# Cosine-similarity attention on one core: norm sums of Q and K folded together on TensorE, the first pair taken head by head, new instruction orders

## The chip, the core and the metric

The kernel runs on one core of a Trainium2 chip. A core has five engines that run side by side, each through its own list of instructions in order: TensorE (PE, matrix products into PSUM), VectorE (DVE), ScalarE (ACT, functions such as the exponential), GpSimd (POOL) and SyncE (SP, which here only issues transfers). They wait for each other through semaphores. Transfers between HBM and the on-chip SBUF are issued by SP or ScalarE and run on 16 DMA engines. PSUM has eight banks of 512 float32 columns for 128 partitions. The metric is the time of one execution in microseconds, lower is better.

## The reference

Inputs Q, K, V are float32 of shape (8, 12, 512, 64): 8 batches, 12 heads, 512 rows of 64 numbers. tau is 0.1.

```python
Q_norm = Q / (np.linalg.norm(Q, axis=-1, keepdims=True) + 1e-10)
K_norm = K / (np.linalg.norm(K, axis=-1, keepdims=True) + 1e-10)
scores = np.einsum('bhqd,bhkd->bhqk', Q_norm, K_norm) / tau
weights = np.exp(scores - np.max(scores, axis=-1, keepdims=True))
weights = weights / (np.sum(weights, axis=-1, keepdims=True) + 1e-10)
return np.einsum('bhqk,bhkd->bhqd', weights, V).astype(np.float32)
```

Scores are cosines divided by 0.1, so they lie between -10 and 10 and the exponential needs no maximum taken off.

## The kernel before

The 96 heads are worked in 48 pairs. A head's 512 rows are laid out as 128 partitions with four rows each; these four blocks are counted t or c from 0 to 3. For a pair s:

- **Load**: Q, K and V, 256 KB each (pair 0's Q and K in halves by head). SP issues them, and for pair 0 ScalarE issues K.
- **Squares** of Q and K in one tile of 16 rows of 64 per partition. From pair 4 on GpSimd squares Q and K together in 1024 columns (L325); pairs 0 to 3 use ScalarE and GpSimd.
- **Sums of squares.** For K, TensorE adds eight products with the identity, each taking 8 of the 64 columns of the eight rows, so that 64 columns are left in PSUM (L342), and VectorE reduces these to 8 sums (L349). For Q, from pair 4 on, VectorE reduces 512 columns to 8 sums itself (L353). Pairs 1 to 3 use TensorE for both, pair 0 VectorE.
- **Inverse roots.** For pairs 0 to 3 ScalarE takes a logarithm and the exponential of minus half of it (L236, L240, L367, L370). Later pairs are taken in groups of 2 or 4, for which VectorE makes Newton steps in some eight small operations (L377 to L386).
- **Products**: Q by its inverse roots on VectorE, K on GpSimd, for ten pairs on VectorE too (L404). Eight **transposes** on TensorE (L410) and one copy on VectorE (L417) give `qt`.
- **Scores**: for each block c of K two matmuls of 512 columns, one per head, into two of the four score banks (L446). **Exponentials**: one ScalarE instruction of 1024 columns per block, with the factor 1/tau as its scale, into `et` (L469). The two pairs of banks take turns, so a score waits for the exponential before the previous one.
- **Values**: V is cast to bf16 with a column of ones (L474); 32 matmuls of 65 columns give the sums and the denominators (L486); VectorE takes a reciprocal and a product (L497, L499), SP stores 256 KB (L503).

For pair 0 each step is made for each head by itself, up to half-size exponentials for blocks 0 and 1. For pair 47 the last block's exponential comes in three pieces (`PIECES`: head 0 whole, head 1's blocks 0 and 1, head 1's blocks 2 and 3; L460), and each piece has its own values, reciprocal, product (L514, L525, L527) and store (L531).

The order is written out by hand. Each operation is added to a list with its engine, what it needs and a due time, and `ORDER` gives, for each engine, the operations' numbers in the order in which it carries them out. Due times had a part in finding the orders; when the kernel is built only `ORDER` counts. An engine's instructions wait for what they need and hold up all that stand behind them in the same list. A negative number in TensorE's list is a matmul without use (L188) of so many columns, and eight others (L185) come first.

Of the kernel before, what the change touches and what calls it, by code (L numbers as in the profile page):

```python
# [8 lines left out]
class Op:  # L9
    def __init__(self, key, eng, kind, due, needs, emit, slot=None):  # L10
        self.key, self.eng, self.kind, self.due, self.emit = key, eng, kind, due, emit
        self.needs, self.slot = [n for n in needs if n is not None], slot
        self.own = False
        self.sem, self.val, self.inc, self.used = None, 0, 0, False
        self.start = self.end = None


class Program:


    def __init__(self, nc):
        self.nc, self.ops, self.list = nc, {}, []

    def add(self, key, eng, kind, due, needs, emit, **kw):
        assert key not in self.ops, key
        op = Op(key, eng, kind, due, needs, emit, **kw)
        self.ops[key] = op
        self.list.append(op)
        return op

# [7 lines left out]
    def dummy(self, columns):  # L38
        return Op("dummy", "pe", "", 0, [], lambda e: self.fill(e, columns))

    def run(self):
        nc = self.nc
        order = self.schedule()
        dma_sems, dma_count, last_out = {}, {}, {}
        for e, ops in order.items():
            for o in ops:
                o.waits = [self.ops[n] for n in o.needs]
                if e in ("pe", "act") and not o.own:
                    o.waits = [p for p in o.waits if p.eng != e]
                for p in o.waits:  # L50
                    p.used = True
        for e, ops in order.items():
# [14 lines left out]
        def write(engine, name):  # L67
            seen = {}
            for o in order[name]:
                want = {}  # L70
                for p in o.waits:
                    k = id(p.sem)
                    if p.val > max(seen.get(k, 0), want.get(k, (None, 0))[1]):
                        want[k] = (p.sem, p.val)
                for k, (sem, val) in want.items():
                    engine.wait_ge(sem, val)
                    seen[k] = val
# [29 lines left out]
def bass_cosine_similarity_attention_kernel(  # L107
# [15 lines left out]
    R_QK, R_V, R_SQ, R_QN, R_QT, R_ET, R_O, R_X = RINGS  # L123

# [13 lines left out]
    xs = {g: sb(f"xs{g}", [128, 64], f32) for g in NORM_ON_ACT}  # L138
# [9 lines left out]
    t_k0 = sc_ps[:, 3, :].bitcast(bf16)[:, 0:SEQ].rearrange("p (t x) -> p t x", t=NT)  # L148
    n_ps = nc.alloc_psum_tensor("nps", [128, R_X, 160], f32)

    P = Program(nc)

# [20 lines left out]

    P.add("one", "pool", "one", -100, [], lambda e: e.memset(ones[:, :], 1.0))
    P.add("eye", "pool", "sm_pool", -99, ["one"], lambda e: e.affine_select(  # L175
        out=ident[:, :], in_=ones[:, :], pattern=[[1, 128]], base=0, channel_multiplier=-1,
        compare_op=ALU.is_equal, fill=0.0))
    P.add("eps", "pool", "sm_pool", -98.5, [], lambda e: e.memset(eps[:, :], 1e-19))
    P.add("table", "act", "table", -900, [], lambda e: e.preload_act_table_set("natural_log_exp_and_others"))
    P.add("vone", "pool", "vone", -98, [], lambda e: e.memset(  # L180
        vb[:, :, :, :, DIM : DIM + 1].rearrange("p r c h o -> p (r c h o)"), 1.0))

    def warm(e):
        for k in range(WARM):
            last = e.matmul(out=o_ps[1][:, :], lhsT=ident[:, :], rhs=warm_in[:, :], start=True, stop=True)  # L185
        return last

    P.fill = lambda e, n: e.matmul(out=sc_ps[:, 0, 0:n], lhsT=ident[:, :], rhs=warm_in[:, 0:n], start=True, stop=True)  # L188
    P.add("wz", "dve", "sm_dve", -100, [], lambda e: e.memset(warm_in[:, :], 0.0))
    P.add("warm", "pe", "warm", -100, ["eye", "wz"], warm)  # L190

    def due_sq(s):
        g = group[s]
        return START + PERIOD * first[g] - 7.6 + (1.9 if g in NORM_ON_ACT else 0) - 3.43 * (first[g] + sizes[g] - 1 - s) - slack(s, M_SQ)

    def due_red(s):
        return due_sq(s) + 2.0

    slots = sorted((START + PERIOD * (s + 1) + 0.9 * PV_AT[4 * h + 3] + 0.05 + late(s), s, h) for s in range(NP - 1) for h in range(2))
    session, attached, early = {}, {}, []  # L200
    for s, w in sorted(((s, w) for s in range(NP) for w in range(2) if on_pe(s, w)), key=lambda j: (due_red(j[0]), j)):
        at = due_red(s) + 0.3
        if s < EARLY:
            early.append((s, w))
            continue
        due, i, h = next(x for x in slots if x[0] >= at and (x[1], x[2]) not in attached)
        attached[i, h] = (s, w)
        session[s, w] = (h, due, [("PV", i, h, NT - 1)])
    before = [[], []]
    for s, w in sorted(early):  # L210
        session[s, w] = (w, due_red(s), before[w])
        before[w] = [("RED", s, w)]
    bank_free = {}
    for s in range(NP):
        for h in range(2):
            bank_free[s, h] = before[h]
            before[h] = [("NRM", s, h)] + ([("RED",) + attached[s, h]] if (s, h) in attached else [])

    def head0(TF):
        for h in range(2):  # L220
            at = -100 + h
            x4 = [xs[0][:, 8 * w + 4 * h : 8 * w + 4 * h + 4] for w in range(2)]
            for w in range(2):
                src_, dst = qk[0][:, w, h, :], sq[0][:, 8 * w + 4 * h : 8 * w + 4 * h + 4, :]
                flat = dst.rearrange("p g d -> p (g d)")
                if SQ0[w][h] == "act":
# [467 lines left out]
```

## Time and profile before

| what | value |
|---|---|
| median of three runs | 190.92 us (190.64 to 191.05) |
| span of the profiled execution | 188.7 us |
| what lies between that span and the median | 2.2 us |
| first exponential starts | 8.08 us |
| busy: ScalarE, TensorE, VectorE, GpSimd | 182.1, 176.0, 164.9, 155.0 us |
| exponentials (L469) | 193 in 175.8 us |
| data moved | 50.75 MB, mean 269 GB/s |

The span runs from the first to the last instruction of one profiled execution; the runs that give the median were not profiled. The execution that was profiled has no other time on record than its span. In the timeline, rows begin with start and duration in microseconds, then engine, line, operation, output and inputs; equal instructions in a row are merged. What stands in brackets is idle time of the engine before the row and what ended it. Matmuls and exponentials overlap their successors, so the distance between starts tells more than the durations.

### The profile page before, as it was taken

What the parts mean: (1) busy time and instruction counts of PE and PEld (TensorE: products, weight loads), DVE (VectorE), ACT (ScalarE), POOL (GpSimd) and SP (SyncE); (2) the same over time, 40 slices, a digit from 0 to 9 for tenths busy, and PEclk for the clock granted to TensorE, in tenths of its full rate; (3) what the DMA queues carried; (4) which work ended last, traced back from release to release, by engine and by line L of the source; (5) the groups of instructions that cost most, each with busy time, mean ns of one, the idle gap of its engine ahead of it and who ended that gap; (6) DMA issues with size and microseconds to landing.
All of it is one profiled execution on the core that took longest, in us unless ns stands there. A gap on an engine that the chain in (4) does not pass through costs nothing.

```text
span 188.7 us, 6679 instructions
## 1 busy us (share of the span) xinstructions
PE 176.0 (93%) x2726; PEld 110.1 (58%) x2726; DVE 164.9 (87%) x530; ACT 182.1 (96%) x214; POOL 155.0 (82%) x145
## 2 busy tenths in 40 slices
PE   6998999999999999999999999999999999899992
PEld 2555666566665666566666566665666556555552
DVE  2789999999999899999999989998889987977543
ACT  4899999999999999999999999999999999999992
POOL 5689999999999999999999899999699898260000
PEclk9999999999999999999999999999999999999999
DMA  4999999999999978999898997997999943113133
GB/s 153 345 352 351 349 357 322 311 315 377 381 385 354 296 264 261 349 335 299 270 255 256 378 344 233 300 314 223 280 326 336 326 139 113 59 56 115 56 114 111
DMA packets 52445, 50.75 MB, mean 269 GB/s; under 512 B 3136, under 2 KB 52416, under 8 KB 52416
## 3 DMA queue, kind: packets, MB, share of 16 engines
q1 hardware_dynamic: 51984, 50.02, 81.6%
q8 instruction: 21, 0.34, 0.7%
q10 hardware_dynamic: 432, 0.33, 0.5%
q14 instruction: 8, 0.07, 0.1%
HBM read 37.75 MB, written 12.58 MB: 267 GB/s over the span
## 4 chain that ended last, share of the span: by engine, by line
ACT 94%; DMA 3%; SPq 1%; issue 1%; DVE 1%; PE 0%
ACT et L469 92%; DMA qk<-in_Q_dram 3%; SPq L299 0%; SPq L296 0%; ACT et L460 0%; DVE ob L527 0%; ACT sq L317 0%; ACT ys L367 0%; ACT nps L370 0%; PE ops L514 0%; DVE rd L525 0%
## 5 line engine op out<-in xcount | busy, mean ns | idle before, releaser
L469 ACT ACTIVATE et<-scps 128x1024 bf16<-128x1024 f32 (+1 forms) x193 | 175.8, 1247 | 0.0
L325 POOL TENSOR_TENSOR sq<-qk 128x1024 bf16<-128x1024 f32 x44 | 82.7, 1891 | 2.0 <-DMA qk<-in_K_dram 2.0
L446 PE MATMUL scps<-qt 64*128 64x512 bf16 x384 | 75.5, 385 | 7.4 <-ACT et L469 2.3
L486 PE MATMUL ops<-vb,et 128*128 128x65 bf16 x1504 | 74.5, 194 | 0.0
L486 PEld LDWEIGHTS ops<-vb,et 128*128 128x128 bf16 x1504 | 56.1, 98 | 27.9 <-issue 21.5
L404 POOL TENSOR_TENSOR qn<-qk,rk 128x512 bf16<-128x512 f32 x37 | 38.1, 1041 | 6.4 <-DVE rk L382 6.1
L499 DVE TENSOR_TENSOR ob<-ops,rd 128x256 f32<-128x256 f32 x94 | 39.3, 420 | 0.9
L404 DVE TENSOR_TENSOR qn<-qk,nps 128x512 bf16<-128x512 f32 x57 | 38.1, 678 | 0.4 <-ACT nps L370 0.4
L417 DVE COPY qt<-tps 128x1024 bf16<-128x1024 bf16 x47 | 32.3, 688 | 4.1 <-PE tps L410 3.4
L446 PEld LDWEIGHTS scps<-qt 64*128 64x128 bf16 x384 | 19.4, 92 | 26.1 <-ACT et L469 10.1
L410 PE MATMUL tps<-ident,qn 128*128 128x128 bf16 x376 | 33.0, 221 | 0.1
L474 POOL TENSOR_SCALAR vb<-vf 128x512 bf16<-128x512 f32 x48 | 29.3, 624 | 0.7 <-PE tps L410 0.7
L353 DVE TENSOR_REDUCE nps<-sq 128x8 f32<-128x512 bf16 x44 | 29.7, 683 | 0.0
L410 PEld LDWEIGHTS tps<-ident,qn 128*128 128x128 bf16 x376 | 21.4, 98 | 12.0 <-issue 5.7
L497 DVE RECIPROCAL rd<-ops 128x4 f32<-128x4 f32 x94 | 16.6, 177 | 9.2 <-PE ops L486 5.8
L342 PE MATMUL ops<-sq,ident 128*128 128x64 bf16 x400 | 20.0, 193 | 0.0
L342 PEld LDWEIGHTS ops<-sq,ident 128*128 128x128 bf16 x400 | 14.9, 98 | 4.1 <-issue 2.9
L349 DVE TENSOR_REDUCE nps<-ops 128x8 f32<-128x64 f32 x44 | 9.3, 211 | 0.8 <-PE ops L342 0.7
L377 DVE TENSOR_TENSOR nps<-nps,ys 128x32 f32<-128x32 f32 (+1 forms) x30 | 6.3, 208 | 0.2
L378 DVE SCALAR_TENSOR_TENSOR nps<-nps,ys 128x32 f32<-128x32 f32 (+1 forms) x30 | 6.2, 207 | 0.2
L185 PE MATMUL ops<-warm_in,ident 128*128 128x512 bf16 x8 | 3.6, 631 | 1.4 <-POOL ident L175 1.4
L319 POOL TENSOR_TENSOR sq<-qk 128x512 bf16<-128x512 f32 (+1 forms) x4 | 3.7, 933 | 1.2 <-DMA qk<-in_K_dram 1.0
(50 smaller groups left out, 40.8 us busy)
## 6 DMA issues: line engine op xcount, KB each, us to landing
vf<-in_V_dram SPq DMA_DIRECT2D x48, 256.0 KB, 5.3
qk<-in_Q_dram SPq DMA_DIRECT2D x47, 256.0 KB, 4.3
qk<-in_K_dram SPq DMA_DIRECT2D x47, 256.0 KB, 5.4
out_dram<-ob SPq DMA_DIRECT2D x47, 256.0 KB, 3.5
qk<-in_Q_dram SPq DMA_DIRECT2D x2, 128.0 KB, 2.7
qk<-in_K_dram ACTq DMA_DIRECT2D x2, 128.0 KB, 2.9
out_dram<-ob SPq DMA_DIRECT2D x1, 128.0 KB, 1.7
out_dram<-ob ACTq DMA_DIRECT2D x1, 64.0 KB, 1.6
```

The source lines that it names most:

```text
L325: lambda e: e.tensor_tensor(out=sqf, in0=data, in1=data, op=ALU.mult))
L342: last = e.matmul(out=o_ps[bank][:, 320:384], lhsT=ident[:, :], rhs=sq[iqs][:, 8 * w : 8 * w + 8, 8 * k : 8 * k + 8], start=(k == 0), stop ...
L353: lambda e, w=w, dst=dst: e.tensor_reduce(out=dst, in_=sq[iqs][:, 8 * w : 8 * w + 8, :], axis=AX.X, op=ALU.add))
L404: lambda e, w=w, r=r: e.tensor_tensor(out=qn[iqn][:, w].rearrange("p t h d -> p h t d"), in0=qk[iq][:, w].rearrange("p h (t d) -> p h t d" ...
L410: last = e.transpose(t_ps[:, w, t, :], qn[iqn][:, w, t].rearrange("p h d -> p (h d)"), ident[:, :])
L417: lambda e: e.tensor_copy(out=qt[iqt][:, :, :, :].rearrange("p w t x -> p (w t x)"), in_=t_ps[:, :, :, :].rearrange("p w t x -> p (w t x)")))
L446: last = e.matmul(out=sc_ps[:, 2 * b + h, :], lhsT=qt[iqt][64 * h : 64 * h + 64, 1, c, :], rhs=qt[iqt][64 * h : 64 * h + 64, 0, :, :], sta ...
L469: lambda e, c=c, b=b, hs=hs: e.activation(out=et[iet][:, c, hs[0] : hs[-1] + 1, :], in_=sc_ps[:, 2 * b + hs[0] : 2 * b + hs[-1] + 1, :], f ...
L474: lambda e: e.tensor_scalar(out=vb[:, iq, :, :, 0:DIM].rearrange("p c h d -> p h c d"), in0=vf[iv][:, :, :].rearrange("p h (c d) -> p h c ...
L486: last = e.matmul(out=o_ps[h][:, 65 * t : 65 * t + 65], lhsT=et[iet][:, c, h, 128 * t : 128 * t + 128], rhs=vb[:, iq, c, h, :], start=(c = ...
L497: lambda e, h=h, grid=grid: e.reciprocal(out=rd[io][:, h, :], in_=grid[:, :, DIM]))
L499: lambda e, h=h, grid=grid: e.tensor_tensor(out=ob[io][:, h], in0=grid[:, :, 0:DIM], in1=rd[io][:, h, :].unsqueeze(2).to_broadcast([128, N ...
```

## The change

- **Sums of squares**: for all pairs from 2 on, TensorE adds sixteen products with the identity, each taking 4 of the 64 columns of all sixteen rows of Q and K, and VectorE makes one reduction of 64 columns to 16 sums. The reductions of 512 columns on VectorE are gone. Pair 1, and pair 0 but for head 0's Q, keep eight products for each sum.
- **Pair 0**: head 0 first. Its Q's square is in two halves, on VectorE and ScalarE; its Q is multiplied by the roots and transposed in halves. Its K is only cast to bf16 and transposed as it is (`raw`); the cast multiplies K by 10 (1 over tau), and K's inverse root enters as the scale of the exponentials, one number per partition. Head 0's first block has two exponentials of 256 columns, the other three one of 512 each; head 1 has two of 1024, of two blocks each. Pair 1 is also written in this way (`EARLY`).
- **Loads**: of pair 0 only head 0's K stays on ScalarE's queue, head 1's K goes to SP as the third load; K of pair 1 goes to ScalarE's queue, behind the table load.
- **Products of K** on VectorE for 20 pairs instead of ten. The square of pair 5 is on VectorE.
- **Order**: all of `ORDER` is new. The matmuls without use are gone, but for the first eight, which now take their weights from a zeroed tile and so don't wait for the identity. On ScalarE the square of pair 1's Q stands ahead of the first exponential, that of pair 2's Q behind four of pair 0's seven. In pair 47 ScalarE takes the last block's pieces in the order head 0, head 1 first half, head 1 second half; before, head 1's first half came first. VectorE handles head 1's first half, head 0, head 1's second half, as before.
- **Waits** that other waits imply are left out.

```diff
-                    for k in range(8):
-                        last = e.matmul(
-                            out=o_ps[bank][:, 320:384], lhsT=ident[:, :], rhs=sq[iqs][:, 8 * w : 8 * w + 8, 8 * k : 8 * k + 8],
-                            start=(k == 0), stop=(k == 7))
+            for k in range(16):
+                last = e.matmul(
+                    out=o_ps[bank][:, 320:384], lhsT=ident[:, :], rhs=sq[iqs][:, :, 4 * k : 4 * k + 4],
+                    start=(k == 0), stop=(k == 15))
...
-                P.add(("RED", s, w), "dve", "red", due_red(s) + 0.5 * w, [*sqs, ("NRMS", 0, 0, 1), *new(g - R_X), *last_direct(s)],
-                      lambda e, w=w, dst=dst: e.tensor_reduce(
-                          out=dst, in_=sq[iqs][:, 8 * w : 8 * w + 8, :], axis=AX.X, op=ALU.add))
+        P.add(("RED", s), "dve", "redp", [("SSQ", s)] + ([] if acts else [*free["n"], *new(g - R_X)]),
+              lambda e: e.tensor_reduce(
+                  out=x2[:, :, c8 : c8 + 8], in_=o_ps[bank][:, 320:384].rearrange("p (w g e) -> p w g e", w=2, e=4), axis=AX.X, op=ALU.add),
...
+                scale = xs[s][:, 16 + 8 + 4 * hs[0] + cs[0] : 16 + 8 + 4 * hs[0] + cs[0] + 1] if one else inv_tau
+                return e.activation(out=o, in_=i, func=ACT.Exp, scale=scale)
...
+                    emit = lambda e, o_=o_, i_=i_: e.tensor_scalar(out=o_, in0=i_, scalar1=inv_tau, scalar2=1.0, op0=ALU.mult, op1=ALU.mult)
+                kind, needs = "cast", lds
...
+EARLY = {0: {'heads': True,
+     'queue': {(0, 0): 'sp', (1, 0): 'act', (0, 1): 'sp', (1, 1): 'sp'},
...
+     'items': (((0,), (0,), 0, 256, 0),
+               ((0,), (0,), 256, 512, 1),
+               ((0,), (1,), 0, 512, 2),
+               ((0,), (2,), 0, 512, 3),
+               ((0,), (3,), 0, 512, 0),
+               ((1,), (0, 1), 0, 512, 2),
+               ((1,), (2, 3), 0, 512, 0))},
+ 1: {'heads': False,
...
+     'queue': {0: 'sp', 1: 'act'},
...
-K_ON_DVE = (1, 2, 3, 4, 9, 15, 21, 27, 33, 39)
+K_ON_DVE = (2, 3, 4, 6, 9, 11, 13, 15, 17, 19, 21, 23, 25, 27, 29, 31, 33, 35, 37, 39)
...
+ ('SQ', 5, 2): 'dve'}
...
     "act": (
-        "9 10 3 12 25 16 18 17 29 31 67 30 68 106 44 74 75 40 41 45 112 47 113 49 82 150 84 151 86 88 120 122 124 126 "
+        "9 4 62 14 24 16 17 30 64 31 38 48 43 39 54 56 70 50 71 117 52 60 121 122 58 81 157 79 158 85 83 129 131 "
...
-        "1717 1719 1747 1749 1751 1753 1781 1783 1785 1788 1787 1789 1804 "
+        "1616 1669 1671 1673 1675 1696 1698 1700 1702 1723 1725 1727 1729 1750 1752 1754 1756 1757 1758 1773 "
```

In the first line of the new ScalarE list 64 is the square of pair 1's Q, 48 the first exponential, 117 the square of pair 2's Q; at the end 1756 to 1758 are the three pieces, which were 1787 to 1789.

## The prediction

> **What bounds the kernel now.** The page first, its busy times and the chain that ended last.
>
> ```profile
> PE 176.0 (93%) x2726; PEld 110.1 (58%) x2726; DVE 164.9 (87%) x530; ACT 182.1 (96%) x214; POOL 155.0 (82%) x145
> ACT 94%; DMA 3%; SPq 1%; issue 1%; DVE 1%; PE 0%
> ```
>
> ScalarE (ACT) carries 94% of the chain. Busy shares on TensorE mislead: its rows overlap. Then the chain in order of time.
>
> ```profile
> 2.67 4.85 DMA qk<-in_Q_dram
> 7.55 0.63 ACT sq L317
> 8.18 0.48 ACT et L469
> ...
> 14.79 169.56 ACT et L469 x185
> 184.34 0.78 ACT et L460 x2
> 185.12 0.05 issue
> 185.16 0.31 PE ops L514 x4
> ```
>
> The middle has no gap: 185 exponentials, 169.56 / 185 = 0.917 us each, from 14.79 to 184.34. Nothing shortens that stretch unless an exponential gets cheaper. A change can gain before 14.8 and after 184.3, and it can lose in between by making ScalarE wait. So I read the head and the tail in the timeline, ScalarE alone.
>
> ```profile
> 6.06 0.63 ACT L317 ACTIVATE sq<-qk 128x512 bf16<-128x512 f32 x1
> 6.60 0.16 ACT L240 ACTIVATE nps<-ys 128x4 f32<-128x4 f32 x1
> 6.83 0.42 ACT L317 ACTIVATE sq<-qk 128x256 bf16<-128x256 f32 x1
> 7.55 0.63 ACT L317 ACTIVATE sq<-qk 128x512 bf16<-128x512 f32 x1 [0.30 <-DMA qk<-in_Q_dram]
> 8.08 0.58 ACT L469 ACTIVATE et<-scps 128x512 bf16<-128x512 f32 x1
> 8.56 0.30 ACT L367 ACTIVATE ys<-xs,eps 128x16 f32<-128x16 f32 x1
> 8.89 0.19 ACT L370 ACTIVATE nps<-ys 128x16 f32<-128x16 f32 x1
> ```
>
> The first exponential starts at 8.08, behind squares that wait for loads: Q of pair 1 (below: Q1) is in at about 6.04, its K (K1) at 6.81, Q of pair 2 at 7.52 (single events of the trace). Starts give each operation's pitch: a square of 512 columns 0.54 (6.06 to 6.60), a 512-column exponential 0.48 (8.08 to 8.56), a logarithm 0.20 but 0.33 when its own root follows at once (8.56 to 8.89), a root 0.11, a 1024-column exponential 0.90, a 256-column one 0.26 (183.98 to 184.24). Pair 1's first exponential starts at 12.55; from there both kernels have the same ScalarE work.
>
> For the end, the timeline of VectorE:
>
> ```profile
> 184.95 0.17 DVE L525 RECIPROCAL rd<-ops 128x2 f32<-128x2 f32 x1 [0.72 <-PE ops L514]
> 185.15 0.29 DVE L527 TENSOR_TENSOR ob<-ops,rd 128x128 f32<-128x128 f32 x1
> 185.50 0.18 DVE L525 RECIPROCAL rd<-ops 128x4 f32<-128x4 f32 x1
> 185.71 0.42 DVE L527 TENSOR_TENSOR ob<-ops,rd 128x256 f32<-128x256 f32 x1
> 186.06 0.16 DVE L525 RECIPROCAL rd<-tps 128x2 f32<-128x2 f32 x1
> 186.25 0.29 DVE L527 TENSOR_TENSOR ob<-tps,rd 128x128 f32<-128x128 f32 x1
> ```
>
> The first reciprocal and product belong to head 1's first piece, whose exponential ran first of the last three; they are over before the last exponential's results arrive, and only two of the three pieces stand behind it.
>
> **The sums, VectorE and GpSimd.** In the groups, 44 reductions of Q on VectorE go (L353, 683 ns each, 29.7 us busy). Ten more K products come to VectorE (L404, 678 ns, 6.8 us), one 1024-column square (about 1.2 by the same row), and GpSimd loses ten products of 1041 ns and that square (1891). VectorE ends some 20 us lighter, GpSimd 12 us. (A pair's one remaining reduction reads 64 columns as before, 211 ns.) Neither is on the chain, so worth nothing on the path; the cover is the unbroken row of exponentials.
>
> **The sums, TensorE.** Eight sum matmuls per pair become sixteen, spaced 0.029 in the trace: +0.23 per pair. TensorE's need per pair by spacing: four score pairs 0.32 each, 32 value matmuls at 0.030, eight transposes at 0.056, eight sums: 2.9 of 3.67 us (four exponentials); it becomes 3.15. On average it fits, but a score may only start once ScalarE has freed its banks, so what counts is the work put between two scores: 0.917 - 0.32 = 0.59 per gap, beyond which scores run late. By rows, a score pair starts 0.06 after the exponential that frees its banks, takes 0.39, the next starts 0.04 later and lasts at least 1.03: 1.52 of two periods (1.83), so 0.32 of lateness is free. Counting the new list, gap by gap: the old had no gap over 0.59; the new one has some of 0.94. Before pair 4's first score stand 12 + 20 value matmuls (0.94), eight transposes (0.45), then 32 sum matmuls (0.93): lateness 0.35, 0.20, 0.53. That is 0.2 over. Four other places reach 0.35, 0.03 over each, inside the error. Taken +0.20; bounds 0 (sums ready early, weights counted high) and +0.45 (each of the waits on VectorE in those gaps adding 0.05).
>
> **The head.** What the new lists do on ScalarE after the loads: half of the first head's Q square, K's square, logarithm, root, logarithm of K, then the 512-column square of pair 1's Q, root, logarithm of head 1, first exponential (256 columns). The first scores need only head 0: Q's logarithm at about 4.3, root 4.6, products and two copies on VectorE (0.29 to 0.42 each) to 6.2, score to 6.5. So the square, in line ahead, decides: first exponential = Q1's landing + 0.02 + 0.54 + 0.11 + 0.20 = landing + 0.87. Q1 is now fourth on SP's queue, behind K's second half (128 KB, 0.35 us at the 358 GB/s of the stretch from 5.6 to 8 us), and K1 leaves SP for ScalarE's queue, where its issue (0.47) stands behind the table load (1.28) and is over by 3.0, ahead of the first data at 3.39. Bounds of the landing: 5.6 (the 220 GB/s between 3.5 and 5.6 filled by the second queue) and 6.81 (Q1 and K1 both in only when the second was before). Taken 6.2, half the 0.35 after 6.04, nearest to the row of the same transfer. First exponential 7.07, 1.0 earlier.
>
> From there to pair 1's first exponential ScalarE does 2 x 0.26 + 3 x 0.48 + 2 x 0.90 of exponentials, two roots 0.22, pair 1's logarithm and root 0.31, the square of pair 2's Q 0.54 (it stood before the first exponential), pair 2's logarithm and root 0.44 back to back: 5.27, where the old had 12.55 - 8.08 = 4.47. So 7.07 + 5.27 = 12.34: the gain shrinks from 1.0 to 0.21. Bounds -0.5 (landing 5.6; then pair 3's norms, whose loads end near 10.75, are late next) and +0.4. What could break the row: K's square for pair 1 on GpSimd (1.04) and head 1's K product (0.61) behind it, 6.81 + 1.65 = 8.5 at the latest; transposes and copy to 9.4, needed at about 10. The raw K costs one cast on GpSimd (about 0.4) instead of a product, its root is an operand of five exponentials; I take no price for that.
>
> The semaphore waits left out as implied, and the fill matmuls (L188), cost nothing on the chain.
>
> **The tail.** The new list runs head 0's exponential first, then head 1's two pieces, but VectorE still normalises head 1's first piece first. That piece is in 0.26 before the last, its reciprocal about 0.33 after its end (as 185.11 to 185.50 with four matmuls, here two), that is 0.06 after the last end, and 0.42 later head 0's reciprocal: 0.48 after, against 185.50 - 185.39 = 0.11 now. All that follows (products, stores on SP) shifts by +0.37. Bounds 0.1 (the last store waiting for the one before it on SP) and 0.45.
>
> **Sum.** -0.21 + 0.20 + 0.37 = +0.36 on the span of 188.7. The three runs' median is 190.92, 2.2 above that span; I carry this over: 191.3. A change of 0.2% (0.38 us) is about what a measurement can tell from none, so this stands at the edge.
>
> **Rivals.** (1) Q1 lands late. For: the two queues shared the engines in turn for pair 0 (landings 3.39, 3.58, 3.94, 4.22, SP and ScalarE alternating). If Q1 and K1 share likewise, Q1 lands near 6.8, +0.6: 191.9. Against: in that stretch the engines were only 0.69 busy.
> The Trainium skill ("DMA: Bandwidth & Descriptors", section "Queues, rings and completion order") says each engine goes round-robin between the queue rows it has work for; by that rule Q1 and K1 finish together and the sum is this rival's. The alternating landings agree with it.
> (2) TensorE stays slow longer. The eight first matmuls take 0.43 us each (3.60 for the row below) and only at about 5.2 the fills' spacing halves.
>
> ```profile
> 1.44 3.60 PE L185 MATMUL ops<-warm_in,ident 128*128 128x512 bf16 x8 [1.44 <-POOL ident L175]
> 4.82 0.78 PE L188 MATMUL scps<-warm_in,ident 128*128 128x256 bf16 x4
> ```
>
> Without fills the speed-up may come a like stretch later, near 9: two single scores (0.21 each) and late transposes, about +0.5: 191.8.
> The Trainium skill ("TensorE: Matmul & The Clock Gate", section "What's actually happening") has the clock released after a busy window that runs freely, which no row here can place.
> (3) Head hides it: the landing is early or pair 4's score in time: 190.9, no change.
> (4) Faster: the pace itself. Exponentials start 0.903 apart while ScalarE is fresh (from 14.66 on) and settle at 0.917; if that is VectorE's traffic, 20 us less of it could give 0.91: 185 x 0.007 = 1.3, so 190.0. It decides below 0.913. Against: from 100 to 180 us VectorE and GpSimd are already lighter, and the pace is the same 0.917.
> (5) The change's lists stall elsewhere (TensorE waiting for sums or products in line before a score): 0.3 each, 192 and more.
>
> **Chances.** Forecast 0.40 (191.0 to 191.6, half on each side of the 0.2% bound), (1) 0.17, (2) 0.08, (3) 0.18, (4) 0.10, (5) 0.07. Faster 0.10; same 0.20 + 0.18 = 0.38; slower 0.52. The range 190.4 to 192.3 leaves out most of (4) and (5).
>
> **What would show it.** First exponential near 7.1 and pair 1's first near 12.3; 46 groups of 16 sum matmuls; a start held back by TensorE near 23 us; after the last exponential the first L525-like reciprocal of head 0 at +0.5 instead of +0.1. Wrong if exponentials show idle time in several places, if their pace differs from 0.917, or if Q1 lands outside 5.6 to 6.8.

## The result and the profile after

The changed kernel takes 200.46 us (median of four runs, 199.59 to 201.24), the kernel before 190.97 beside it (190.64 to 191.05): 1.0500 times as long, 95% interval 1.0469 to 1.0532. The forecast was 191.3, from 190.4 to 192.3. It was wrong by 9 us. Some executions of a kernel came out 1.5% or more above its fastest; each time below is the median of the others, with their range. The profiled execution of the changed kernel took 201.24 us with a span of 199.5, against 188.7 before: 10.8 us to be found.

From its page, the busy times, the chain by engine, and the group of the exponentials (busy time, mean ns of one, then idle time before them and what ended it):

```profile
PE 184.7 (93%) x3097; PEld 121.4 (61%) x3097; DVE 157.5 (79%) x508; ACT 186.0 (93%) x215; POOL 141.9 (71%) x132
PE 42%; ACT 33%; DMA 9%; POOL 6%; DVE 5%; SPq 2%; issue 1%; POOLq 0%
L288 ACT ACTIVATE et<-scps 128x1024 bf16<-128x1024 f32 x192 | 178.5, 1034 | 6.2 <-PE scps L270 5.2
```

ScalarE had 94% of the chain and has 33%; TensorE, with only 8.7 us more of busy time than before, leads. ScalarE now waits 5.2 us for scores where its row had no gap, and its busy time grew by 3.9 us: exponentials that start late overlap less.

The chain in order of time, the changed kernel:

```profile
2.16 4.04 DMA qk<-in_Q_dram
6.22 0.63 ACT sq L320
...
24.87 18.60 ACT et L288 x20
45.13 0.47 PE ops L651 x12
...
69.64 1.05 PE ops L531 x32
71.01 0.59 PE ops L651 x16
71.93 0.60 PE ops L651 x16
...
121.83 4.19 DMA qk<-in_K_dram
126.16 1.90 POOL sq L321
128.05 1.01 POOL qn L618
129.83 0.47 PE ops L651 x12
...
158.24 4.20 DMA vf<-in_V_dram
162.51 0.62 POOL vb L638
163.13 1.01 POOL qn L618
166.13 29.43 ACT et L288 x33
```

It can be read in three stretches. The exponentials bind in short stretches to about 50 us. Then groups of work on TensorE (sums L531, values L651) stand in the chain one after another, each between two scores. From about 108 us the chain leaves TensorE and goes back through GpSimd to loads: a K load ends before a square, and right behind that square a K product goes off; the same again with a V load and its cast. From 166 us ScalarE is unbroken to the end.

How far the same exponential ends later than in the kernel before (two profiled executions, worked out from single instructions) puts sizes to the stretches. I call this the lag. After 1, 5, 13, 23, 35, 37, 41 and 47 pairs it is 0.28, 1.04, 1.59, 3.19, 5.85, 8.82, 10.31 and 10.44 us; the tail adds 0.34. So some 5.5 us are lost slowly up to pair 35, and 4.5 in a few steps between pairs 35 and 41. The granted clock was 0.50 from 146.0 to 149.4, inside the largest of these steps (2.74 us at one pair); the last section comes back to this.

The head and the end of ScalarE, timeline of the changed kernel:

```profile
6.22 0.63 ACT L320 ACTIVATE sq<-qk 128x512 bf16<-128x512 f32 x1 [0.61 <-DMA qk<-in_Q_dram]
7.04 0.47 ACT L288 ACTIVATE et<-scps,xs 128x256 bf16<-128x256 f32 x1
7.41 0.17 ACT L409 ACTIVATE nps<-ys 128x4 f32<-128x4 f32 x1
7.67 1.27 ACT L288 ACTIVATE et<-scps,xs 128x512 bf16<-128x512 f32 x2
8.82 0.30 ACT L392 ACTIVATE ys<-xs,eps 128x16 f32<-128x16 f32 x1
...
11.96 1.92 ACT L288 ACTIVATE et<-scps 128x1024 bf16<-128x1024 f32 x2
...
194.49 1.34 ACT L288 ACTIVATE et<-scps 128x512 bf16<-128x512 f32 x3
```

Pair 1's Q landed at 6.20 (forecast 6.2), the first exponential starts at 7.04 (7.07). But the second of the two at 11.96, pair 1's first, starts at 12.86, not 12.34. The exponentials that read their scale from xs take longer: two of 512 columns from 7.67 to 8.82 are 0.58 each, where the row before had 0.48; the one of 256 takes 0.37 from start to start (7.04 to 7.41) against 0.26. Five of them: about 0.5.

The end on VectorE:

```profile
195.88 0.17 DVE L694 RECIPROCAL rd<-ops 128x2 f32<-128x2 f32 x1 [1.14 <-PE ops L683]
196.08 0.29 DVE L696 TENSOR_TENSOR ob<-ops,rd 128x128 f32<-128x128 f32 x1
196.29 0.17 DVE L694 RECIPROCAL rd<-ops 128x4 f32<-128x4 f32 x1
```

The last exponential ends at 195.83 (194.49 + 1.34); head 1's first piece is divided at +0.05 and head 0's reciprocal starts at +0.46, as forecast (0.06 and 0.48).

The waits of the changed kernel, microseconds in total, times, longest:

```profile
POOL vb L638 <- DMA vf<-in_V_dram: 12.0, 5, 6.7
POOL sq L321 <- DMA qk<-in_K_dram: 9.9, 11, 2.0
PEld tps L625 <- POOL qn L618: 5.6, 9, 1.8
ACT et L288 <- PE scps L270: 5.2, 10, 2.0
```

The row of the squares before, from pair 4 on:

```profile
POOL sq L325 <- DMA qk<-in_K_dram: 2.0, 5, 0.7
```

With the first pairs, which the row of the changed kernel includes, it was 4.6 us against 9.9, and V's loads were not among the leading waits. Both lists of SP put the loads of pair s behind the store of pair s - 12 (V: s - 9).

### The profile page after: what moved, and what is told of

Its sections match the earlier page's. It is cut to its first block, busy times and chain, and to the rows that moved or that the text cites. A ratio compares the mean times of both kernels' runs of the same rounds, so it can differ in the third digit from the quotient of the medians.

```text
span 199.5 us, 7412 instructions
## 1 busy us (share of the span) xinstructions
PE 184.7 (93%) x3097; PEld 121.4 (61%) x3097; DVE 157.5 (79%) x508; ACT 186.0 (93%) x215; POOL 141.9 (71%) x132
## 4 chain that ended last, share of the span: by engine, by line
PE 42%; ACT 33%; DMA 9%; POOL 6%; DVE 5%; SPq 2%; issue 1%; POOLq 0%
ACT et L288 33%; PE scps L270 14%; PE ops L651 13%; PE tps L625 8%; PE ops L531 6%; DMA qk<-in_K_dram 5%; POOL sq L321 3%; DMA vf<-in_V_dram 2%; POOL qn L618 2%; DMA qk<-in_Q_dram 2%; POOL vb L638 1%; DVE ob L662 1%; DVE qn L618 1%; SPq L496 1%; DVE qt L630 1%
## 5 line engine op out<-in xcount | busy, mean ns | idle before, releaser
L288 ACT ACTIVATE et<-scps 128x1024 bf16<-128x1024 f32 x192 | 178.5, 1034 | 6.2 <-PE scps L270 5.2
L321 POOL TENSOR_TENSOR sq<-qk 128x1024 bf16<-128x1024 f32 (+2 forms) x48 | 85.6, 1796 | 13.7 <-DMA qk<-in_K_dram 9.9
L270 PE MATMUL scps<-qt 64*128 64x512 bf16 (+1 forms) x383 | 75.8, 388 | 4.3 <-ACT et L288 2.7
L651 PE MATMUL ops<-vb,et 128*128 128x65 bf16 x1504 | 72.0, 195 | 1.1 <-ACT et L288 1.0
L651 PEld LDWEIGHTS ops<-vb,et 128*128 128x128 bf16 x1504 | 55.6, 98 | 28.1 <-issue 18.9
L618 DVE TENSOR_TENSOR qn<-qk,nps 128x512 bf16<-128x512 f32 x66 | 44.0, 676 | 0.3 <-ACT nps L558 0.2
L618 POOL TENSOR_TENSOR qn<-qk,rk 128x512 bf16<-128x512 f32 x26 | 26.8, 1044 | 10.7 <-DVE rk L571 9.1
L531 PE MATMUL ops<-sq,ident 128*128 128x64 bf16 x736 | 29.0, 192 | 0.1
L531 PEld LDWEIGHTS ops<-sq,ident 128*128 128x128 bf16 x736 | 24.4, 97 | 7.0 <-issue 3.8
L539 DVE TENSOR_REDUCE nps<-ops 128x16 f32<-128x64 f32 x44 | 9.9, 230 | 11.0 <-PE ops L531 10.2
L571 DVE SCALAR_TENSOR_TENSOR nps<-nps,ys 128x16 f32<-128x16 f32 (+1 forms) x28 | 5.1, 181 | 0.1
L223 PE MATMUL ops<-warm_in 128*128 128x512 bf16 x8 | 3.6, 631 | 1.2 <-DVE warm_in L211 1.2
```

The source lines that it names most:

```text
L270: last = e.matmul(out=sc_ps[:, b + i, 0 : hi - lo], lhsT=qt[iqt][64 * h : 64 * h + 64, 1, c, :], rhs=qt[iqt][64 * h : 64 * h + 64, 0, :, : ...
L288: return e.activation(out=o, in_=i, func=ACT.Exp, scale=scale)
L321: return lambda e: e.tensor_tensor(out=b, in0=a, in1=a, op=ALU.mult)
L531: last = e.matmul(out=o_ps[bank][:, 320:384], lhsT=ident[:, :], rhs=sq[iqs][:, :, 4 * k : 4 * k + 4], start=(k == 0), stop=(k == 15))
L539: lambda e: e.tensor_reduce(out=x2[:, :, c8 : c8 + 8], in_=o_ps[bank][:, 320:384].rearrange("p (w g e) -> p w g e", w=2, e=4), axis=AX.X, ...
L618: lambda e, w=w, r=r: e.tensor_tensor(out=qn[iqn][:, w].rearrange("p t h d -> p h t d"), in0=qk[iq][:, w].rearrange("p h (t d) -> p h t d" ...
```

## What the two theories were

**Theory T, TensorE's gaps.** The forecast let 0.59 us of work stand between two scores (0.917 - 0.32). The trace of before already showed otherwise: from the start of the last value matmul of a group to the first score after it lie 0.125 us (tenth percentile, 88 cases between 40 and 160 us), where value matmuls follow each other at 0.029; behind a transpose 0.151 against 0.056. So every change from other work to a score costs about 0.095 more. A gap holds 0.50, not 0.59. The spacings 0.029 and 0.056 are medians; in the mean value matmuls follow each other at 0.032, transposes at 0.058, sums at 0.030. With these the need per pair is 3.23 + 4 x 0.095 = 3.61 of 3.67 us, and a recount of the new list, gap by gap, gives some 30 places beyond the free 0.32 of lateness and 3.7 us; the old list none. The sum is steep: with 0.030 for a value matmul, as in the prediction, it is 2.1. In the changed kernel a gap that is too full looks like this:

```profile
69.25 0.39 PE L270 MATMUL scps<-qt 64*128 64x512 bf16 x2
69.57 1.12 PE L531 MATMUL ops<-sq,ident 128*128 128x64 bf16 x32
70.62 0.39 PE L270 MATMUL scps<-qt 64*128 64x512 bf16 x2
```

From score to score lie 1.37 us, 0.45 more than an exponential's 0.917.

**Rival R, the lists.** GpSimd's new list has K products that are due behind squares of pairs up to seven further on and V casts of pairs up to five further on (in the old list six and three). These wait for loads, the loads stand behind stores on SP, and the stores wait for the values, which a late TensorE gives late. Then it is the loads, whatever TensorE's work.

## The experiments

**Half the sums.** The changed kernel with 8 products per sum.

```diff
-            for k in range(16):
+            for k in range(8):
...
-                    start=(k == 0), stop=(k == 15))
+                    start=(k == 0), stop=(k == 7))
```

> The changed kernel with 8 of the 16 sum matmuls of each pair; half of each norm's sum is left out, all other instructions and all lists stay. Theory T (TensorE is too full between two scores: every change from other work to a score and back costs 0.095 us beside the matmuls, so a gap holds 0.50 us of work, not 0.59; the late loads of the second half are a consequence): with 0.23 us per pair less, the count of gaps leaves about 0.3 of the 3.7 to 4.7 us of lateness, and the late loads go with it: 190.97 + 0.28 (head) + 0.35 (tail) + 0.3 = 191.9, between 191.5 and 194. Rival R (the lists themselves: V casts ahead of K products on GpSimd and loads behind stores on SP, whatever TensorE has to do): 198 to 200.

Measured 198.01 us (197.81 to 199.17), 1.0369 times before (1.0323 to 1.0414). T's 191.9 is far off, and the time is R's. But the trace splits: the lag is 0.83 after five pairs and 0.86 after 13 (changed kernel: 1.04 and 1.59), so the slow loss does go; then it jumps to 1.58, 3.27, 6.28 and 7.00 (23, 35, 37, 47 pairs). Its chain:

```profile
85.85 4.33 DMA qk<-in_K_dram
90.18 0.59 POOL vb L638
90.78 1.55 issue
92.32 1.90 POOL sq L321
94.22 1.18 POOL vb L638 x2
95.40 1.01 POOL qn L618
97.17 0.60 PE ops L651 x16
```

A K load, squares and casts behind it, and last the K product for which TensorE waits. The late loads are no mere consequence of TensorE's lateness.

**Loads ahead of the stores.** The changed kernel, each store held back by three stores in SP's list.

```diff
+        sp = order["sp"]
+        moved, held = [], []
+        for o in sp:
+            if o.key[0] == "ST" and o.key[1] < 44:
+                held.append(o)
+                if len(held) > 3:
+                    moved.append(held.pop(0))
+            else:
+                moved.append(o)
+                if o.key[0] == "LV" and o.key[1] == 47:
+                    moved += held
+                    held = []
+        order["sp"] = moved + held
```

> The changed kernel with each store three stores later in SP's list, so that loads stand ahead of them. Theory T: only the late part goes (pairs 35 to 41, where the chain passes late K and V loads, 3 to 4.5 us): 195.5 to 197.5; the lag of the exponentials at pair 31 stays at 4 to 5 us. Rival R: the loads are the cause of all of it: 191.3 to 192.5, lag at pair 31 below 1.

Measured 198.8 (two executions, 198.64 and 198.99). The time misses both, by a fault of the experiment: stores of pairs 41 to 43 went out 18 to 24 us after their exponentials, and the span ends 6.3 us behind the last exponential, 2.6 more than in the changed kernel. Less these 2.6 us it would be 196.2, as T said. The exponentials tell what was asked: lag 3.35 after 23 pairs, 4.94 after 35 and after 37, 5.21 at the end. The steps late in the kernel are gone and most of the slow loss is still there.

**A constant scale.** The changed kernel, pair 0's head 0.

```diff
-                scale = xs[s][:, 16 + 8 + 4 * hs[0] + cs[0] : 16 + 8 + 4 * hs[0] + cs[0] + 1] if one else inv_tau
+                scale = 0.1 if one else inv_tau
```

> The changed kernel with a constant scale in the five exponentials of pair 0's head 0, in place of the root of K's norm read from memory; the norm of that head's K is left out of the result. If the operand costs 0.11 us in each: pair 1's first exponential at 12.86 - 5 x 0.11 = 12.3, the forecast's 12.34. If the longer pitch is from something else (their place after loads, the half widths): 12.86 as before. The whole time moves by 0.5 or less either way, since later lateness may take it up: 199.9 to 200.5.

The pitch fell from 0.586 to 0.494 (512 columns) and from 0.368 to 0.274 (256): the operand costs 0.09 in each. Pair 1's first exponential still came at 12.99, for in that execution Q of pair 1 landed at 6.55, 0.35 later, and the first exponential started at 7.40. From there to pair 1 it is 5.59 against 5.82 in the changed kernel; the rest of the 0.46 went into waits (from root to exponential 0.27 instead of 0.17, and 0.23 instead of 0.12). Whole time 202.22 (201.45 to 204.02), above the 199.9 to 200.5 expected: no gain to be seen in it.

**Twice the sums in the old lists.** The kernel before.

```diff
-                    for k in range(8):
+                    for k in [*range(8), *range(8)]:
```

> The kernel before with each of K's eight sum matmuls made twice, the second row of them beginning the sum anew, so that TensorE has the changed kernel's 16 per pair in the old lists. Theory T: by the count of gaps 14 places over 0.50 us, +1.2 us: 192.2, more (to 194) if late loads follow. By the forecast's own capacity of 0.59 per gap: no place over it, 0.0, 190.9 to 191.1. Rival R (only the new lists matter): 191.0.

193.64, 1.0142 times before (1.0100 to 1.0184): the forecast's capacity (0.0) and R (no loss) fall. 0.76 of the lag is there after one pair, from the first pairs' sums in the head; 1.84 come slowly afterwards (0.76 to 2.60), against 1.24 counted.

So both theories hold a part. The second series asks whether the two parts add up to the whole.

**Both undone.** The changed kernel with 8 products, and SP's order as follows, which gives the stores their old place after the last load.

```diff
+        moved, held, more = [], [], True
+        for o in order["sp"]:
+            if o.key[0] == "ST" and more:
+                held.append(o)
+                if len(held) > 3:
+                    moved.append(held.pop(0))
+            else:
+                moved.append(o)
+                if o.key == ("LV", 47):
+                    moved, held, more = moved + held, [], False
+        order["sp"] = moved
```

> The changed kernel with 8 of 16 sum matmuls (half of each norm's sum left out) and with each store three stores later in SP's list until the last load, then in its old place. Theory now: two causes that add, TensorE's gaps (10.44 - 6 = about 4 to 5 us of lag) and loads that stand behind stores (about 5 to 6). With both taken away the exponentials' lag behind the kernel before ends at 0.9 to 1.3 us, of which 0.4 to 0.5 in the head; with the tail's 0.35: 192.1 to 192.7. If there is a third cause in the lists (GpSimd or VectorE themselves too late): 194 or more.

192.38 (192.17 to 192.51), ratio 1.0062 (1.0041 to 1.0082), as forecast. The lag is 0.74 after five pairs and 1.19 at the end. The chain by engine on its page:

```profile
ACT 89%; PE 5%; DMA 2%; DVE 1%; SPq 1%; issue 0%
```

ScalarE binds again. A third large cause is not there.

**Loads ahead alone**, with the same edit of SP's order and all 16 products.

> The changed kernel, all 16 sums, with each store three stores later in SP's list until the last load, then in its old place (in a2_loads_ahead three stores were held to the end, which lengthened the tail by about 2.6 us). Lag of the exponentials 5.2 at the end as in a2_loads_ahead, tail 0.35: 190.97 + 5.2 + 0.35 = 196.5, between 195.9 and 197.2.

196.26 (196.12 to 196.34), ratio 1.0259 (1.0239 to 1.0279); lag 4.75 after 35 pairs and 5.03 at the end. Waits of GpSimd in it:

```profile
POOL qn L630 <- DVE rk L583: 20.9, 11, 7.0
POOL sq L333 <- DMA qk<-in_K_dram: 3.7, 3, 1.6
```

V's loads are no longer among its leading rows, and GpSimd now waits for norms, 20.9 us; with both undone it waits 18.0 us for them, and ScalarE binds all the same. So loads behind stores are worth 200.46 - 196.26 = 4.2 us, and the eight more sums 196.26 - 192.38 = 3.9 us when no load is late. By the lag at the end it is 10.44 - 5.03 = 5.4 (the profiled execution of the changed kernel is the longest of its four) and 5.03 - 1.19 = 3.84.

**Products ahead in GpSimd's list.** The changed kernel; each K product from pair 20 on moves ahead of up to six squares and casts of later pairs.

```diff
+        pool = order["pool"]
+        for o in [o for o in pool if o.key[0] == "SCL" and o.key[1] >= 20]:
+            k = pool.index(o)
+            to = k
+            while k - to < 6 and (pool[to - 1].key[0] == "SQ" and pool[to - 1].key[1] > o.key[1] + 3 or pool[to - 1].key[0] == "VC" and pool[to - 1].key[1] > o.key[1]):
+                to -= 1
+            pool.insert(to, pool.pop(k))
```

> The changed kernel with each of GpSimd's K products from pair 20 on moved ahead of up to six squares and V casts of pairs further on; SP's list as it is. Theory: late loads cost time because products that are due stand in line behind squares and casts of pairs 5 to 9 further on, which wait for their loads; then the late part (pairs 35 to 41, 4.5 to 5 us) goes: 195.5 to 197.5. If the loads are late for what needs them themselves: 199 to 201, as the changed kernel.

205.61 (204.11 to 205.78), slower still: a miss. GpSimd's wait for norms rose to 35.6 us (9.1 in the changed kernel), in stretches of up to 6.7 us: the norms come in groups of four pairs, the moved products stood waiting for them, and the squares of the next group waited behind the products. Changing the order moved the wait to another place in line, so this does not tell what was asked.

**Scores over all rows.** The kernel before, from pair 1 on.

```diff
-                            out=sc_ps[:, 2 * b + h, :], lhsT=qt[iqt][64 * h : 64 * h + 64, 1, c, :],
-                            rhs=qt[iqt][64 * h : 64 * h + 64, 0, :, :], start=True, stop=True)
+                            out=sc_ps[:, 2 * b + h, :], lhsT=qt[iqt][64 * h * (s == 0) : 64 * h + 64 if s == 0 else 128, 1, c, :],
+                            rhs=qt[iqt][64 * h * (s == 0) : 64 * h + 64 if s == 0 else 128, 0, :, :], start=True, stop=True)
```

> The kernel before with scores over all 128 rows of K and Q from pair 1 on, so that each head's score holds both heads' sums. If the 0.095 us at each change from other work to a score is the price of going from weights over all rows to weights over 64: the spacing from the last value matmul to the first score falls from 0.125 to about 0.03, and the two scores, 0.003 apart now, follow each other at about 0.21. If it belongs to the score as such (its banks, the wait before it): 0.125 stays.

TensorE's timeline near 61 us, first the kernel before, then this one:

```profile
60.38 0.41 PE L486 MATMUL ops<-vb,et 128*128 128x65 bf16 x8
60.72 0.39 PE L446 MATMUL scps<-qt 64*128 64x512 bf16 x2
61.04 0.34 PE L410 MATMUL tps<-ident,qn 128*128 128x128 bf16 x3
```

```profile
60.91 0.41 PE L486 MATMUL ops<-vb,et 128*128 128x65 bf16 x8
61.16 0.59 PE L446 MATMUL scps<-qt 128*128 128x512 bf16 x2
61.59 0.22 PE L410 MATMUL tps<-ident,qn 128*128 128x128 bf16 x1
```

Eight value matmuls and then a score: 0.34 from first to score before, 0.25 here. Over 40 to 160 us the spacing falls from 0.125 to 0.029, and behind transposes from 0.151 to 0.056. The price belongs to the change from weights over 128 rows to weights over 64, not to the score, its banks or its waits. The two scores, 0.003 apart before, now follow at 0.215. What side by side saves in them (0.43 to 0.32) the change of form takes back but for a little: 0.32 + 0.125 before, 0.43 + 0.029 here. The Trainium skill ("TensorEngine Tiling", section "Key Properties") says that a change of the tiling mode drains TensorE, and gives no size. The trace agrees in that a change to 64 rows takes time, 0.096 here; a drain itself it does not show. The one execution of this kernel took 192.2 us, 1 us more than before beside it, nearly all of it in one step near 113 us whose cause was not looked for.

**Fourteen sums.** As the kernel with loads ahead alone, with 14 products.

```diff
-            for k in range(16):
+            for k in range(14):
...
-                    start=(k == 0), stop=(k == 15))
+                    start=(k == 0), stop=(k == 13))
```

> c2_loads_ahead with 14 of the 16 sum matmuls (an eighth of each norm's sum left out). Counting gap by gap with 0.095 us per change to a score gives 1.92 us of steady lateness where 16 give 3.66 and 8 give 0.33; so against c2_loads_ahead -1.74: 194.5, and 1.6 above c1_half_sums_loads_ahead: 194.1. In proportion to the matmuls left out it would be 196.26 - 0.25 x 3.78 = 195.3; by a capacity without the 0.095, 0.29 against 0.65: 195.9.

194.62 (194.23 to 194.80), ratio 1.0183 (1.0151 to 1.0216). The loss is not in proportion to the work: the last two of eight more matmuls cost 196.26 - 194.62 = 1.64, the six before them 194.62 - 192.38 = 2.24. By the lag at the end (5.03, 3.17, 1.19) it is 1.86 and 1.98; in proportion it would be 0.96 and 2.88. The count with 0.095 said 1.74 and 1.59. A capacity without it said 0.36 for the last two.

**Head and tail undone too.** As both undone, with the constant scale and the last pieces in the old order.

```diff
-                scale = xs[s][:, 16 + 8 + 4 * hs[0] + cs[0] : 16 + 8 + 4 * hs[0] + cs[0] + 1] if one else inv_tau
+                scale = 0.1 if one else inv_tau
...
-        "1616 1669 1671 1673 1675 1696 1698 1700 1702 1723 1725 1727 1729 1750 1752 1754 1756 1757 1758 1773 "
+        "1616 1669 1671 1673 1675 1696 1698 1700 1702 1723 1725 1727 1729 1750 1752 1754 1757 1756 1758 1773 "
```

> c1_half_sums_loads_ahead with, beside it, the constant scale in pair 0's head 0 (that head's K norm and half of each norm's sum left out) and, as in the kernel before, head 1's first piece as the first of the last three exponentials. The tail gives 0.33 back, the scale about 0.3 to 0.5: 192.48 - 0.33 - 0.4 = 191.75, between 191.3 and 192.0; the 0.7 us of lag between pairs 3 and 15 stays. If the head's lag is from something else: 192.1.

191.74 (191.30 to 192.12), ratio 1.0024 (1.0000 to 1.0048), as expected. Lag 0.07 after the first pair, 0.51 after five, 0.95 at the end.

**Loads ahead in the kernel before**, with the same edit of SP's order.

> The kernel before with each store three stores later in SP's list until the last load. Theory: its GpSimd waits 2.0 us in all for K's loads and is never late for TensorE, so loads further ahead are worth nothing: 190.8 to 191.2. If the loads behind stores cost in every list: faster by 0.5 or more.

190.96 (190.60 to 191.50), ratio 0.9998 (0.9981 to 1.0015). The same loads behind the same stores cost nothing under the old lists.

The traces of both kernels show what differs (worked out from single instructions, pairs 18 to 45, medians). From the landing of a load to the moment at which GpSimd is done with all that stands ahead of its use pass 10.0 us for a V cast and 2.7 us for a square in the kernel before, 4.4 and 0.35 us in the changed one; there 14 of 56 loads land too late, before 2. With 8 sums it is 3.9 and 0.35. The stores do not go later behind their pair's last exponential (pairs 6 to 35: 4.5 us in the mean, before 5.1). So it is not a late TensorE that delays the loads, which rival R had thought part of it: GpSimd, with fewer products and with casts further ahead in its list, comes to them sooner.

**The square of pair 2's Q later.** The kernel before.

```diff
+        for e, o, to in (("act", ("SQ", 2, 0), ("EXP", 0, 0, 0)), ("pe", ("SSQ", 2, 0), ("SCO", 0, 1, 1)), ("dve", ("RED", 2, 0), ("EVA", 1))):
+            x = self.ops[o]
+            order[e].remove(x)
+            order[e].insert(order[e].index(self.ops[to]) + 1, x)
```

> The kernel before with the square of pair 2's Q moved from ahead of the first exponential to behind the second (its sums and reduction moved likewise on TensorE and VectorE). The first score ends at 7.80, so the first exponential starts at 7.84 instead of 8.08; the ScalarE work up to pair 1 stays the same sum: -0.24, 190.7 to 190.8. If pair 2's norms or the later scores of pair 0 hold it up: 191.0 or more.

193.95 (193.22 to 194.24; ratio 1.0139, 1.0111 to 1.0166): a miss of 3 us. ScalarE's timeline:

```profile
10.47 1.07 ACT L473 ACTIVATE et<-scps 128x512 bf16<-128x512 f32 x2
13.47 0.31 ACT L371 ACTIVATE ys<-xs,eps 128x16 f32<-128x16 f32 x1 [1.92 <-DVE xs L353]
```

ScalarE stands for 1.92 us before pair 2's logarithm, which the list puts ahead of an exponential. I had moved the square and its sums, but not the logarithm, and on TensorE the sums now stood ahead of pair 0's third score. It is the same error as in the forecast, made in the head: a step was priced by its own time and not by what is in line behind it.

**Which loads.** With two more runs: only Q's and K's loads moved ahead, or only V's, each from pair 18 on. The edit, here for Q and K (the other has `("LV",)`):

```diff
+        q = []
+        for o in order["sp"]:
+            if o.key[0] == "ST":
+                q.append(("s", o))
+            elif o.key[0] in ("LD",) and o.key[1] >= 18:
+                k = len(q)
+                n = 0
+                while k > 0 and n < 3:
+                    if q[k - 1][0] == "s" or q[k - 1][0] == "o":
+                        n += q[k - 1][0] == "s"
+                        k -= 1
+                    else:
+                        break
+                q.insert(k, ("m", o))
+            else:
+                q.append(("o", o))
+        order["sp"] = [o for _, o in q]
```

> The changed kernel with the loads of Q and K from pair 18 on three stores earlier in SP's list, those of V left. In the changed kernel's chain K's loads end two waits (before the squares at 126.2 and 143.2) and V's one (before the cast at 162.5), some 1.5 us each. If each load holds up only its own place: about two thirds of the 4.2 us go, 197.6 (197 to 198.5). If V's alone are late enough to keep the whole: 200.0 or more. If K's alone: 196.3.

> The changed kernel with the loads of V from pair 18 on three stores earlier in SP's list, those of Q and K left. By the same account a third of the 4.2 us goes: 199.0 (198 to 199.6). If K's loads alone are the cause: 200.5. If V's: 196.3.

V's alone: 196.91 (three executions, 196.85, 196.91 and 199.67, the last at a mean clock of 0.986, the others at 0.999 and 0.995). In the profiled execution (196.91) the late steps are gone, lag 5.84 after 35 pairs and 6.12 at the end, although GpSimd still waits 16.3 us for K's loads. Q's and K's alone: 203.39 (200.86 to 203.79), slower. Moving them put V's loads of the pairs about 15 behind four more transfers: V of pair 15 landed at 52.7 where it had been 50.6. GpSimd there:

```profile
52.82 0.63 POOL L656 TENSOR_SCALAR vb<-vf 128x512 bf16<-128x512 f32 x1 [2.03 <-DMA vf<-in_V_dram]
53.40 1.04 POOL L636 TENSOR_TENSOR qn<-qk,rk 128x512 bf16<-128x512 f32 x1
```

Right behind the cast that waited comes a K product, and the lag goes from 1.27 after 11 pairs to 6.33 after 13. A V load that lands 2.1 us later, at a place that waited 0.52 us in the changed kernel, is followed by 5 us of loss: a wait in line, as rival R has it, and behind it a granted clock of 0.50 from 54.04 to 60.87. How much of the 5 us is the clock's was not separated. V's loads moved alone give back 3.5 of the 4.2 us in two executions of three, which points to the V casts; what K's loads cost these two runs do not settle, for the spread of both is wide.

## Why the prediction was wrong

- **The sums, TensorE: the step that failed.** "0.917 - 0.32 = 0.59 per gap" left out what a change to a score costs. The need of 2.9 and 3.15 per pair had been put together from spacings of like after like (scores 0.32, values 0.030, transposes 0.056); the spacings between unlike ones, four in each pair, were not read. With 0.096 for each a gap holds 0.50, and value matmuls follow each other at 0.032 in the mean, not 0.030. The term was +0.20 (bounds 0 and 0.45) and measured 3.9 us (3.84 by the lag). That it is the room in a gap and not the matmuls' own time is shown from two sides: the old lists lose 2.6 us with 16 per pair where 0.59 a gap said none, and two of eight matmuls left out give back nearly half. That 0.096 of the room belongs to the change of rows the kernel with scores over all rows shows; that this is what fills the gaps is the count's, which comes near the loss with it (3.7) and not without it (0.5).
- **"GpSimd 12 us ... worth nothing": the second term that was missing.** The sum of an engine's work was taken for its slack. GpSimd does have less to do (13 us), but it comes to its squares and casts sooner, they wait for loads, and products that are due stand behind them, so loads which were harmless before (loads ahead in the old kernel: 0.0) cost 4.2 us. That moving the loads gives this back is shown; that it goes through the products in line is read from the chains, since the run that moved the products did not settle it. VectorE's "some 20 us lighter" was 7.4 in busy time (164.9 to 157.5): its instructions last 19.5 us less in all, but they overlap. Rival (5) named the kind (a stall in line), at 0.3 a place and a chance of 0.07; no list of GpSimd was counted against the landing of its loads.
- **The raw K: "I take no price for that".** Five operands read from memory cost 0.09 each. The head's gain of 0.21 became a loss: after the first pair 0.28 later, where without the operand, in the kernel with all undone, it is 0.07. The other 0.28 lies in the sum of 5.27 for ScalarE's work from the first exponential to pair 1's, which takes 5.61 without the operand too; it left out small waits between the rows. The Trainium skill ("ScalarE: Activation LUTs", section "What ACT_TABLE_LOAD costs") gives about 93 ns for each operand of one value per partition; the trace agrees, 0.368 - 0.274 = 0.094.
- **Right:** Q of pair 1 in at 6.20, the first exponential at 7.04, the tail's +0.37 (0.34 measured between last exponential and end of span). The exact hit on the landing is luck: in the eleven profiled executions with these first loads it lies between 5.84 and 6.55, within the bounds. Rival (1), with Q of pair 1 near 6.8, did not come, nor (2): TensorE's clock rose at 6.06, 0.8 later than before and not near 9. Rival (4), a faster pace with a lighter VectorE: with both undone VectorE is as light as in the changed kernel, and from pair 15 to 47 the lag grows by 0.19, so the pace stays at 0.917.
- **The account by runs:** loads behind stores 4.2, eight more sums 3.9, scale and tail 0.6 (192.38 - 191.74), and 0.8 left over (0 to 0.9 by the ratio's interval), of which the trace shows 0.26 between pairs 3 and 5 and 0.23 near pair 15; their cause was not looked for. The runs are of different series, whose medians of the kernel before lie between 190.91 and 191.21, so each part is known to some 0.3 at best. The parts do not stand alone: eight sums fewer without moving the loads save 2.4 only (200.46 - 198.01).

## What to carry to other kernels

Where a queue must return to a due instruction at fixed times, count the work between two of them, with the spacings between unlike instructions, which a table of like after like does not have; at 98% of the period a tenth of a microsecond per change decides. An engine with less work is not an engine with more slack: it comes to its transfers sooner. In an in-order list look for the due operation that stands behind one that waits for a transfer. And an engine's time given back counts only where the chain passes.

## What the runs showed of the hardware

TensorE's granted clock fell to 0.50 in the middle of several kernels, for 3.413 us (in one case twice that). The windows view of the changed kernel, in steps of 3.413 from the rise of the clock at 6.06 (columns: window, then busy time and instructions of PE, PEld, DVE, ACT, POOL, the granted clock, the DMA share, GB/s):

```profile
139.18:142.59 3.41, 3.21 (x72) 2.29 (x69) 2.59 (x14) 3.22 (x5) 2.49 (x2) 1.00 0.98 331
142.59:146.00 3.41, 1.34 (x16) 0.65 (x16) 2.58 (x6) 2.68 (x3) 2.85 (x3) 1.00 0.89 269
146.00:149.42 3.41, 3.32 (x34) 2.02 (x34) 1.33 (x3) 1.62 (x2) 3.08 (x4) 0.50 0.66 214
```

The drop begins on this grid (146.005 - 6.058 = 41 x 3.413), right behind a window in which TensorE was busy for 0.39 of the time, waiting for a K product. In the 16 profiled executions of this study there are eight such drops, in six kernels, each behind a window busy for 0.39 to 0.55; no window busy for 0.62 or more was followed by one. The longest single idle stretch in those windows was 0.7 to 1.7 us; a window with one of 1.1 us, but busy for 0.67, was not followed by a drop. In the seven drops of one window TensorE was busy for 0.97 of it or more; in the longer one the first window was busy for 0.86 and a second slow one came. So a stall of TensorE is paid twice where it fills half a window: it takes its own length and then half the speed in the next (34 matmuls above, where a full window has 72). In the changed kernel the profiled execution had a mean clock of 0.986 and a span of 199.5, the other three 0.995 to 0.997 and 197.6 to 198.8. One such window takes 0.0086 off the mean (half of 3.413 in 199.5) and a mean of 0.995 leaves 0.005, so the other three ran without it, and with 200.26 as their median time most of the loss is not the clock's. That the drop is the whole difference between them is likely, but their traces were not taken. The Trainium skill ("TensorE: Matmul & The Clock Gate", section "What's actually happening") gives a free-running window of 3413 ns, and the trace agrees with its length. It names an idle window as what lowers the clock; here the measurement differs: no window was idle, and the clock fell behind windows busy for half.
